# Two more merge gate tiles ahead of the first weighted sum, and output tiles that begin with the dense half

## The chip, the cores and the metric

One core of one Trainium2 chip. The metric is the time of one execution in device microseconds, shown as the median of several runs; a profile is one execution of its own. PE is the matmul engine, DVE the vector engine, ACT the scalar engine, POOL and SP the other two; SP mostly issues DMAs.

## What is computed

A decoder trunk of two layers over 512 tokens of width 1024, all in float32. Cut to what matters:

```python
def hybrid_layer(x, ...):
    h = rmsnorm(x, norm_g)
    proj = h @ w_in                       # one projection feeds everything below
    ...
    o_nsa, o_pool, o_conv, o_fox = ...    # four mixers of width 256; two are attentions
    acc = None
    for i, o in enumerate((o_nsa, o_pool, o_conv, o_fox)):
        branch = (o * jax.nn.silu(gates[:, :, i])) @ w_branch[i]
        term = jax.nn.sigmoid(merge[:, :, i]) * branch      # merge: 4 x 1024 columns of proj
        acc = term if acc is None else acc + term
    return x + acc @ w_out

def reference(x, ...):
    for l in range(DEPTH):
        x = hybrid_layer(x, ...)
    return rmsnorm(x, final_norm_g)
```

## The kernel before, in words

**Tiles.** Activations lie with features on the 128 partitions and the 512 tokens along the columns. A weight tile is 128 x 1024: eight blocks of 128 input features for 128 output features, 512 KB. To keep float32 accuracy every operand is held in two parts, a high one and the rest: ACT makes the high part (`split`, L70), DVE the rest (L71, or L74 with a scale), and each product is three matmuls: high times high, high weight times rest, rest of the weight times high. So `dense` (L286) makes one output tile of 128 features by 24 matmuls (L299) into a bank `ps_d` (three of them). The evacuation that it gets as `evac` is put into a background list and runs between later matmuls.

**Weights.** `Stream` (L88) holds the order in which the weight tiles are loaded and used. Raw tiles go into three buffers `wr` by DMAs that SP issues (L168); the split parts lie in `wh` and `wl`, two buffers each. Ahead of the merge, `ws.more()` (L152) lends it more raw buffers: one in the space of the tables `rope`, three in that of `V`, the attention's values.

**A layer in order.** Projections and gates; then 12 attention units, written out by a plan by hand (L1190 on): scores (`S`, L648 and L649), softmax on DVE and ACT (L651 to L663), transposes (`T`, L672), values (`PV`, L694), reading of the bank `ps_o` by ACT and DVE (L717, L718), and at a head pair's end its branch input `y` (L702 to L707). Between these steps `FILL` = 7 matmuls of a generator, `filler` (L1156), are issued: more projections, at the end the merge gates of the first output tile, `for i in range(4)` at L1170. A merge gate tile is a `dense` whose evacuation, `ev_merge` (L807), scales (L320) and applies a tanh on ACT (L813).

**The weighted sum** is made in two ways. The first 512 of its 1024 features, the *dense half*, go tile by tile: `branches(m)` (L818) takes the four gates of tile m, multiplies each by its branch (24 matmuls, L828, into `ps_s` and `ps_pt`; L833, L837) and splits the sum into `st`. The loop at L1212 makes the four gates of tile m, then `branches(m)`; `m` = 0 has had its gates in the filler. The other 512 features come out of `merge` (L951) with the tokens on the partitions, by a scheme that saves matmuls (seven products instead of eight); at its end (L1032 to L1040) PE turns them round by 16 transposes (L1036) and they are split into `y`. Its first weight tiles are prepared ahead.

**The output projection.** Layer 0: for each of eight tiles a `dense` over `(ah, al)`, the eight features of the sum, and the residual added by `ev_out` (L1232). `dense` takes the eight features in order, the high weight's two products first, so its 14 first matmuls need features of the dense half (0 to 3) and of the turned half (4 to 7). The last layer makes the eight tiles twice, for 256 tokens each (L1264 on, `ev_last` L1252), so that the last norm and the stores of the first half of the tokens lie beside the second half's matmuls; its eight weight tiles are loaded and split twice (L105).

**What sets the order.** The program is written in the order above, but the tile framework puts the instructions of each engine into an order of its own at build time, from the dependences, the buffers and its own estimate of times. On the chip each engine works through its list in order. So a change of the source's order moves instructions only as far as that list shows.

## Time and profile before

| | us |
|---|---|
| median of 3 runs | 966.85 |
| lowest and highest | 966.73, 968.93 |
| the profiled execution | 966.74 |
| its span, first to last instruction | 964.9 |
| PE busy | 939.8 (97%) |
| DVE busy | 715.6 (74%) |
| ACT busy | 522.0 (54%) |
| mean granted clock of PE | 0.993 of full |

The busy times are shares of the span; PE's is long because a matmul's end is modelled. "Granted clock" is the share of its 2.4 GHz that PE was given; 0.5 is 1.2 GHz.

### The profile page before, as it was taken

What the parts mean: (1) busy time and instruction counts of PE and PEld (TensorE: products, weight loads), DVE (VectorE), ACT (ScalarE), POOL (GpSimd) and SP (SyncE); (2) the same over time, 40 slices, a digit from 0 to 9 for tenths busy, and PEclk for the clock granted to TensorE, in tenths of its full rate; (3) what the DMA queues carried; (4) which work ended last, traced back from release to release, by engine and by line L of the source; (5) the groups of instructions that cost most, each with busy time, mean ns of one, the idle gap of its engine ahead of it and who ended that gap; (6) DMA issues with size and microseconds to landing.
All of it is one profiled execution on the core that took longest, in us unless ns stands there. A gap on an engine that the chain in (4) does not pass through costs nothing.

```text
span 964.9 us, 12942 instructions
## 1 busy us (share of the span) xinstructions
PE 939.8 (97%) x4728; PEld 797.9 (83%) x4728; DVE 715.6 (74%) x1397; ACT 522.0 (54%) x912; POOL 31.1 (3%) x45
## 2 busy tenths in 40 slices
PE   7999999999999999999999999999998999999896
PEld 5988888888778888887889888888886888888796
DVE  6694689986887677775568549998778868676765
ACT  7295475665644454544327537566655544545363
POOL 0000000000000001000100000000000000000010
PEclk9999999999999999999999999999999999999998
DMA  6253222132254667644514322221312655686253
GB/s 263 78 173 111 86 80 76 57 110 66 66 160 146 166 205 196 187 140 148 188 62 164 120 88 87 66 69 64 109 66 98 192 141 171 211 214 210 70 181 129
DMA packets 39904, 125.81 MB, mean 130 GB/s; under 512 B 4496, under 2 KB 6560, under 8 KB 39840
## 3 DMA queue, kind: packets, MB, share of 16 engines
q1 hardware_dynamic: 36000, 113.43, 35.4%
q0 software_dynamic: 2976, 10.50, 5.5%
q10 hardware_dynamic: 864, 1.05, 0.3%
q8 instruction: 37, 0.61, 0.3%
q14 instruction: 27, 0.22, 0.1%
HBM read 120.77 MB, written 4.19 MB: 130 GB/s over the span
## 4 chain that ended last, share of the span: by engine, by line
PE 93%; DVE 3%; DMA 1%; ACT 1%; issue 1%; POOL 0%; DVEq 0%; SPq 0%; ACTq 0%; POOLq 0%
PE ps_d L299 55%; PE ps_d L984 9%; PE ps_s L984 5%; PE ps_o L694 3%; PE ps_pt L672 2%; PE ps_pt L984 2%; PE ps_s L828 2%; PE ps_pt L1022 2%; PE ps_s L550 2%; PE ps_pt L550 2%; PE ps_s L649 1%; PE ps_pt L828 1%; PE ps_s L648 1%; PE ps_o L1022 1%; PE ps_d L1022 1%; PE ps_o L411 1%
## 5 line engine op out<-in xcount | busy, mean ns | idle before, releaser
L299 PE MATMUL ps_d<-xh,wh 128*128 128x512 f32 x632 | 249.8, 396 | 9.1 <-ACT xh L73 6.7
L299 PE MATMUL ps_d<-xl,wh 128*128 128x512 f32 x632 | 249.7, 395 | 0.0
L70 ACT ACTIVATE wh<-wr 128x1024 fp32r<-128x1024 f32 (+2 forms) x136 | 140.9, 1039 | 170.0 <-PE ps_d L299 76.5
L71 DVE TENSOR_TENSOR wl<-wr,wh 128x1024 fp32r<-128x1024 f32 (+2 forms) x136 | 162.7, 1200 | 48.2 <-ACT wh L70 47.8
L299 PE MATMUL ps_d<-xh,wl 128*128 128x512 f32 x632 | 172.7, 391 | 0.0
L299 PEld LDWEIGHTS ps_d<-xh,wh 128*128 128x128 f32 x632 | 119.6, 189 | 32.8 <-ACT xh L73 6.7
L299 PEld LDWEIGHTS ps_d<-xl,wh 128*128 128x128 f32 x632 | 119.5, 189 | 24.1 <-DVE xl L74 1.2
L299 PEld LDWEIGHTS ps_d<-xh,wl 128*128 128x128 f32 x632 | 117.5, 188 | 23.4
L320 DVE TENSOR_TENSOR t<-ps_d,rstd 128x512 f32<-128x512 f32 x74 | 50.8, 686 | 36.0 <-PE ps_d L299 35.5
L653 ACT ACTIVATE p<-p,nm 128x128 f32<-128x128 f32 (+1 forms) x96 | 53.3, 556 | 26.1 <-DVE nm L651 25.4
L651 DVE CUSTOM_DVE_ANT_0 p<-ps_s,cst 128x128 f32<-128x128 f32 (+1 forms) x96 | 45.3, 484 | 14.4 <-PE ps_pt L672 7.7
L694 PE MATMUL ps_o<-ptx,V 128*128 128x256 f32 (+1 forms) x288 | 49.6, 286 | 2.4 <-DVE o L718 1.6
L70 ACT ACTIVATE ptx<-ps_pt 128x384 fp32r<-128x384 f32 (+1 forms) x72 | 37.0, 520 | 26.6 <-PE ps_o L694 11.9
L694 PEld LDWEIGHTS ps_o<-ptx,V 128*128 128x128 f32 x288 | 42.4, 191 | 6.2 <-DVE o L718 2.2
L71 DVE TENSOR_TENSOR ptx<-ps_pt,ptx 128x384 fp32r<-128x384 f32 (+1 forms) x72 | 42.0, 594 | 2.1 <-ACT ptx L70 2.0
L672 PE MATMUL ps_pt<-cst,p 128*128 128x128 f32 x240 | 40.7, 277 | 1.3 <-DVE ptx L71 0.9
L299 PE MATMUL ps_d<-y,wh 128*128 128x256 f32 (+1 forms) x192 | 40.3, 329 | 0.9 <-ACT y L73 0.9
L299 PE MATMUL ps_d<-st,wh 128*128 128x256 f32 (+1 forms) x192 | 34.2, 321 | 1.3 <-ACT wh L70 1.3
L299 PEld LDWEIGHTS ps_d<-y,wh 128*128 128x128 f32 x192 | 30.6, 197 | 3.7 <-ACT y L73 1.4
L672 PEld LDWEIGHTS ps_pt<-cst,p 128*128 128x128 f32 x240 | 28.2, 141 | 5.6 <-PE ps_o L694 1.3
L71 DVE TENSOR_TENSOR wl<-V,wh 128x1024 fp32r<-128x1024 f32 x18 | 22.0, 1224 | 14.3 <-ACT wh L70 14.1
L299 PEld LDWEIGHTS ps_d<-st,wh 128*128 128x128 f32 x192 | 28.5, 190 | 4.7 <-ACT wh L70 2.1
(341 smaller groups left out, 1725.7 us busy)
## 6 DMA issues: line engine op xcount, KB each, us to landing
wr<-in_w_all_dram SPq DMA_DIRECT2D x145, 512.0 KB, 3.3
V<-in_w_all_dram SPq DMA_DIRECT2D x26, 512.0 KB, 3.8
rope<-in_w_all_dram SPq DMA_DIRECT2D x12, 512.0 KB, 4.2
t<-in_xT_dram SPq DMA_DIRECT2D x16, 256.0 KB, 4.5
V<-in_w_all_dram POOLq DMA_DIRECT2D x8, 512.0 KB, 8.0
wr<-in_w_all_dram SPq DMA_DIRECT2D x8, 400.0 KB, 3.0
wr<-in_w_all_dram POOLq DMA_DIRECT2D x6, 512.0 KB, 6.2
ptc<-in_xT_dram SPq DMA_DIRECT2D x8, 256.0 KB, 3.3
```

The costliest lines, as they stand in the source:

```text
L70: ACT.activation(hi, src, AF.Copy)
L71: DVE.tensor_tensor(lo, src, f32(hi), ALU.subtract)
L299: PE.matmul(acc[:, :width], w, r[k][:, tok], start=(n == 0), stop=(n == 23))
L320: DVE.tensor_tensor(t, acc, state["rb"], ALU.mult)
L550: PE.matmul(accs[tt][:, 0:400], x[:, tt * 128:tt * 128 + 128], w, start=(k == 0 and a == 0), stop=(kp == 3 and kk == 1 and a == 2))
L651: DVE.tensor_tensor_reduce(out=P[:, :n], in0=s[:, :n], in1=bias, scale=1.0, scalar=3e38, op0=ALU.add, op1=ALU.min, accum_out=nm)
L653: ACT.activation(P[:, :n], P[:, :n], AF.Exp, bias=nm, scale=-1.0, accum_out=sm)
L672: PE.transpose(p[:, c:c + 128], self.P[qt][:, kb * 128:kb * 128 + 128], ident)
L694: PE.matmul(dst, V[:, kb, self.vset, :], part[:, src], start=(self.fresh and self.cmp is None and b == 0 and kb == 0 and j == 0), stop=(se ...
L828: PE.matmul(p, w[:, c], r, start=(n == 0), stop=(n == 5))
L984: PE.matmul(bank[tt], x, w[:, d], start=(opens and k == 0 and n == 0), stop=(name in ("P2", "P3", "P4") and k == 3 and n == 2), skip_group ...
L1022: PE.matmul(p, x[:, c], w[:, d], start=(n == 0), stop=(n == 5))
```

## The change

1. **Gates.** `filler` makes six merge gate tiles instead of four (`LOGITS[:4 + AHEAD]`). In the loop, `branches(m)` now comes ahead of the next four gates, so each sum has its gates and two of the following tile behind it; the last sum is preceded by two gates alone. `ws.more()` is called behind the second group of gates. The weight tiles are laid out in that order.
2. **Output tiles.** `dense` gets `early`: the 12 matmuls that need the dense half only come first, all three products, then the other 12. The first two output tiles of each layer are such; their generators (`lead`) are advanced by 12 matmuls each inside `merge`, ahead of the transposes.
3. **The last layer.** Its first two output tiles are made once for all 512 tokens; the other six for 256 at a time, as before. The sum of squares of the two tiles (`sq01`) is kept for both halves. Two weight tiles fewer are loaded.

```diff
--- before.py
+++ after.py
@@ -24,6 +24,8 @@
 ACT_NORM = ()
 HID = (9, 11, 13, 15)
 GATES = [(0, 0), (2, 0), (0, 1), (2, 1), (1, 0), (3, 0), (1, 1), (3, 1)]
+LOGITS = [(m, i) for m in range(4) for i in range(4)]
+AHEAD = 2
 BIG = 1e30
 HEAD_ROWS = (1, 3, 0, 2)
 SWAP = [(i + 8) % 16 if i < 16 else i for i in range(32)]
@@ -102,7 +104,7 @@
                                 self.added.add(len(self.order) - 1)
                     self.order += [(l, o + 9), (l, o + 8)]
                 self.order += [(l, i) for i in range(NTILE - KT, NTILE)]
-            self.order += [(L - 1, i) for i in range(NTILE - KT, NTILE)]
+            self.order += [(L - 1, i) for i in range(NTILE - KT + 2, NTILE)]
             self.n = len(self.order)
             self.loaded = self.done = self.taken = 0
             self.slots = ["wr"] * 3
@@ -283,13 +285,15 @@
                 pass
             bg.pop(0)
 
-    def dense(rhs, evac, tok=slice(0, T)):
+    def dense(rhs, evac, tok=slice(0, T), early=False):
 
         i, (wh, wl) = ws.take()
         drain(2)
         acc = psum("d", 3)
         order = [(a, k) for k in range(7) for a in (0, 1)] + [(2, k) for k in range(7)]
         order += [(a, 7) for a in range(3)]
+        if early:
+            order = [(a, k) for h in (0, 4) for b in ((0, 1), (2,)) for k in range(h, h + 4) for a in b]
         rh, rl = rhs
         width = tok.stop - tok.start
         for n, (a, k) in enumerate(order):
@@ -804,11 +808,11 @@
         yield
 
 
-    def ev_merge(i):
+    def ev_merge(m, i):
 
         def g(acc):
             t = scaled(acc)
-            state["sig"][i] = t
+            state["sig"][m, i] = t
             yield
             ACT.activation(t, t, AF.Tanh, scale=0.5)
             yield
@@ -829,7 +833,7 @@
                     n += 1
             if i == 0:
                 ws.split(i0 + 1)
-            sg = state["sig"][i]
+            sg = state["sig"].pop((m, i))
             DVE.scalar_tensor_tensor(sg, sg, 1.0, p, op0=ALU.add, op1=ALU.mult)
             if tot is None:
                 tot = sg
@@ -948,7 +952,7 @@
         merge_ahead(1)
         return ready.pop(0)
 
-    def merge(l, side, ah, al):
+    def merge(l, side, ah, al, lead):
 
         rth = sb([128, 8], "rth", 1)
         DVE.tensor_scalar(rth[:, 0:4], state["rt"], 0.5, None, op0=ALU.mult)
@@ -1029,6 +1033,13 @@
                         DVE.tensor_tensor(acc[tok], acc[tok], sg, ALU.add)
                     if tok == toks[0]:
                         merge_ahead(2)
+        state["prep"] = None
+        assert not ready
+        ws.slots = [x for x in ws.slots if x == "wr"]
+
+        for g in lead:
+            for _ in range(12):
+                next(g)
 
         for f in range(4):
             pt = psum("pt", 2)
@@ -1038,9 +1049,6 @@
             split(h, lo, pt, scale=0.5)
             ah.append(h)
             al.append(lo)
-        state["prep"] = None
-        assert not ready
-        ws.slots = [x for x in ws.slots if x == "wr"]
 
 
     nc.gpsimd.dma_start(ng, gains)
@@ -1167,8 +1175,8 @@
             yield from dense(rhs, ev_conv("x", 1))
             yield from with_mix(dense(rhs, ev_conv("c", 1)))
             yield from dense(rhs, ev_conv("b", 1))
-            for i in range(4):
-                yield from dense(rhs, ev_merge(i))
+            for m, i in LOGITS[:4 + AHEAD]:
+                yield from dense(rhs, ev_merge(m, i))
 
         def with_mix(d):
             for n, _ in enumerate(d):
@@ -1212,20 +1220,14 @@
         for m in range(4):
             if m == 1:
                 ws.more()
-            if m:
-                for i in range(4):
-                    for n, _ in enumerate(dense(rhs, ev_merge(i))):
-                        if n % 12 == 11 and steps:
-                            next(side)
-                            steps -= 1
             a, b = branches(m)
+            for mi in LOGITS[4 * m + 4 + AHEAD:4 * m + 8 + AHEAD]:
+                for n, _ in enumerate(dense(rhs, ev_merge(*mi))):
+                    if n % 12 == 11 and steps:
+                        next(side)
+                        steps -= 1
             ah.append(a)
             al.append(b)
-        merge(l, side, ah, al)
-        if l + 1 < L:
-            par = load_par(l + 1)
-
-
         if l + 1 < L:
             def ev_out(m, xres):
                 def g(acc):
@@ -1236,34 +1238,54 @@
                     yield
                 return g
 
-            for m in range(KT):
+            def project(m):
                 xres = temp()
                 nc.sync.dma_start(xres, (xT.rearrange("(k p) t -> k p t", p=128) if l == 0 else x1d)[m])
-                run(dense((ah, al), ev_out(m, xres)))
-            drain()
-
-
-    xn = []
-    for m in range(KT):
-        xres = sb([128, T], "xh", 8)
-        nc.sync.dma_start(xres, x1d[m])
-        xn.append(xres)
-
-    def ev_last(m, c):
-        def g(acc):
-            x = xn[m][:, c]
-            DVE.tensor_tensor(x, acc[:, :T // 2], x, ALU.add)
-            add_square(x, m)
-            yield
-            if m < KT - 1:
-                ACT.activation(x, x, AF.Copy, scale=ng[:, 16 + m:17 + m])
-            yield
-        return g
+                yield from dense((ah, al), ev_out(m, xres), early=m < 2)
+        else:
+            xn = []
+
+            def ev_last(m, c):
+                def g(acc):
+                    x = xn[m][:, c]
+                    if m == 2:
+                        state["sq"] = state["sq01"][:, c]
+                    DVE.tensor_tensor(x, acc[:, :c.stop - c.start], x, ALU.add)
+                    add_square(x, m)
+                    if m == 1:
+                        state["sq01"] = state["sq"]
+                    yield
+                    if m < KT - 1:
+                        ACT.activation(x, x, AF.Copy, scale=ng[:, 16 + m:17 + m])
+                    yield
+                return g
+
+            def project(m, half=0):
+                if half == 0:
+                    xres = sb([128, T], "xh", 8)
+                    nc.sync.dma_start(xres, x1d[m])
+                    xn.append(xres)
+
+                c = slice(half * T // 2, half * T // 2 + T // 2) if m > 1 else slice(0, T)
+                yield from dense((ah, al), ev_last(m, c), c, early=m < 2)
+
+        lead = [project(m) for m in range(2)]
+        merge(l, side, ah, al, lead)
+        if l + 1 < L:
+            par = load_par(l + 1)
+
+
+        for g in lead:
+            run(g)
+        for m in range(2, KT):
+            run(project(m))
+        drain()
+
 
     for half in range(2):
         c = slice(half * T // 2, half * T // 2 + T // 2)
-        for m in range(KT):
-            run(dense((ah, al), ev_last(m, c), c))
+        for m in range(2, KT) if half else ():
+            run(project(m, half))
         drain()
         _, rb = stats(T // 2, keep=True)
         x = xn[KT - 1][:, c]
@@ -1355,8 +1377,9 @@
             tiles += [feat(run(s + 128 * h)) for s in (652, 908, 1420, 1164)]
         pairs = lambda m: [m[256 * j:256 * j + 256].reshape(2, 128, 512).transpose(1, 0, 2).reshape(128, 1024)
                            for j in range(len(m) // 256)]
+        logit = [feat(run(3472 + 1024 * i + 128 * m)) for m, i in LOGITS]
         for m in range(4):
-            tiles += [feat(run(3472 + 1024 * i + 128 * m)) for i in range(4)]
+            tiles += logit[4 * m + (AHEAD if m else 0):4 * m + 4 + AHEAD]
             tiles.append(a["w_branch"][l].reshape(8, 128, 1024)[:, :, m * 128:m * 128 + 128]
                          .transpose(1, 0, 2).reshape(128, 1024))
         for bp in range(2):
```

The order of the instructions on an engine, before and now, at three places. In the rows, `xh`, `xl` are the parts of the normalised input, `wh`, `wl` those of a weight tile, `ptx` and `V` probabilities and values, `y` branch inputs (at the output: the turned half of the sum), `st` the dense half of the sum.

**PE, layer 1, behind the last score matmuls** (before: `L648`, `L649` scores, `L828` sums). Before, at the place where the value matmuls of the last two units begin:

```order
L672 MATMUL ps_pt<-cst,p 128x128 x2
L694 MATMUL ps_o<-ptx,V 128x256
L694 MATMUL ps_o<-ptx,V 128x128 x2
L828 MATMUL ps_s<-y,wh 128x512 x3
L828 MATMUL ps_s<-y,wl 128x512
L828 MATMUL ps_s<-y,wh 128x512 x2
L828 MATMUL ps_s<-y,wl 128x512
L672 MATMUL ps_pt<-cst,p 128x128 x2
```

Now, at the same place (`L303` gates, `L832` sums):

```order
L698 MATMUL ps_o<-ptx,V 128x256 x2
L698 MATMUL ps_o<-ptx,V 128x128 x2
L676 MATMUL ps_pt<-cst,p 128x128 x3
L698 MATMUL ps_o<-ptx,V 128x256 x4
L303 MATMUL ps_d<-xh,wh 128x512
L303 MATMUL ps_d<-xl,wh 128x512
L303 MATMUL ps_d<-xh,wl 128x512
L832 MATMUL ps_s<-y,wh 128x512 x2
L832 MATMUL ps_s<-y,wl 128x512
L698 MATMUL ps_o<-ptx,V 128x256 x2
L698 MATMUL ps_o<-ptx,V 128x128 x2
L676 MATMUL ps_pt<-cst,p 128x128 x7
```

Ahead of the first row now stand 21 matmuls of one gate tile, and behind the last row 24 of another; before, no gate tile stood there, only sums.

**PE, the output of the last layer**, from the last matmul row of `merge` on. Before:

```order
L1022 MATMUL ps_pt<-wl,y 128x512
L299 MATMUL ps_d<-st,wh 128x256 x16
L1036 MATMUL ps_pt<-cst,p 128x128 x8
L299 MATMUL ps_d<-y,wh 128x256 x2
L1036 MATMUL ps_pt<-cst,p 128x128 x4
L299 MATMUL ps_d<-y,wh 128x256 x4
L1036 MATMUL ps_pt<-cst,p 128x128 x4
L299 MATMUL ps_d<-y,wh 128x256 x5
L299 MATMUL ps_d<-st,wl 128x256 x4
```

Now:

```order
L1026 MATMUL ps_pt<-wl,y 128x512
L303 MATMUL ps_d<-st,wh 128x512 x8
L303 MATMUL ps_d<-st,wl 128x512 x4
L303 MATMUL ps_d<-st,wh 128x512 x8
L1047 MATMUL ps_pt<-cst,p 128x128 x4
L303 MATMUL ps_d<-st,wl 128x512 x4
L1047 MATMUL ps_pt<-cst,p 128x128 x4
L303 MATMUL ps_d<-y,wh 128x512 x2
L1047 MATMUL ps_pt<-cst,p 128x128 x4
L303 MATMUL ps_d<-y,wh 128x512 x4
L1047 MATMUL ps_pt<-cst,p 128x128 x4
L303 MATMUL ps_d<-y,wh 128x512 x9
```

The two tiles' matmuls with `st` stand ahead of the transposes with all three products, 512 columns wide; before, 16 of 256 columns stood there.

**ACT, layer 1, around the last value matmul.** Before:

```order
L70 ACTIVATE ptx<-ps_pt 128x384
L717 ACTIVATE o<-ps_o 64x512
L705 ACTIVATE y<-o 128x512
L70 ACTIVATE ptx<-V 128x1024
L70 ACTIVATE wh<-wr 128x1024 x2
```

Now:

```order
L72 ACTIVATE ptx<-ps_pt 128x384
L721 ACTIVATE o<-ps_o 64x512
L817 ACTIVATE t<-t 128x512
L709 ACTIVATE y<-o 128x512
L72 ACTIVATE ptx<-V 128x1024
L817 ACTIVATE t<-t 128x512
L72 ACTIVATE wh<-wr 128x1024 x2
```

A tanh (`L817`) now stands between the split of the merge tile in `V` and the splits of the next two gates' weights.

## Rows read from the trace of the kernel before

**Rows 1.** The page: busy time by engine; shares of the chain by engine
```profile
PE 939.8 (97%) x4728; PEld 797.9 (83%) x4728; DVE 715.6 (74%) x1397; ACT 522.0 (54%) x912; POOL 31.1 (3%) x45
...
PE 93%; DVE 3%; DMA 1%; ACT 1%; issue 1%; POOL 0%; DVEq 0%; SPq 0%; ACTq 0%; POOLq 0%
```

**Rows 2.** Table of stretches: us, busy by engine (instructions), PE's granted clock, DMA share, GB/s
```profile
254.51:270.63 16.12, 14.12 (x87) 11.78 (x86) 14.08 (x33) 9.45 (x19) 0.00 (x0) 1.00 0.18 49
270.63:278.66 8.03, 6.02 (x27) 4.23 (x26) 7.12 (x11) 3.28 (x5) 0.00 (x0) 1.00 0.56 198
724.18:740.53 16.35, 14.46 (x78) 11.75 (x77) 13.36 (x32) 8.84 (x18) 0.00 (x0) 0.90 0.16 49
740.53:747.51 6.98, 6.01 (x26) 4.22 (x25) 6.88 (x11) 3.28 (x5) 0.00 (x0) 1.00 0.62 225
431.30:478.37 47.07, 46.13 (x209) 37.52 (x208) 27.84 (x39) 18.72 (x26) 3.84 (x7) 1.00 0.48 162
900.14:954.77 54.63, 51.96 (x413) 50.84 (x412) 36.07 (x58) 30.34 (x50) 3.46 (x3) 0.97 0.42 135
732.60:735.62 3.02, 3.02 (x8) 2.31 (x9) 2.77 (x7) 0.60 (x1) 0.00 (x0) 0.52 0.35 85
906.51:909.43 2.92, 2.92 (x15) 2.92 (x14) 0.89 (x2) 1.19 (x2) 0.00 (x0) 0.50 0.00 0
```

**Rows 3.** Groups by line on PE, 254.5 to 270.62: values and transposes
```profile
L694 PE MATMUL ps_o<-ptx,V 128*128 128x256 f32 (+1 forms) x36 | 6.2, 289 | 1.4 <-DVE o L718 1.3
...
L672 PE MATMUL ps_pt<-cst,p 128*128 128x128 f32 x20 | 3.3, 277 | 0.3 <-DVE ptx L71 0.3
```

**Rows 4.** PE in order of time, steady pieces: start us, us, line and operation, count
```profile
236.26 1.02 PE L694 MATMUL ps_o<-ptx,V 128*128 128x256 f32 x7
237.11 0.62 PE L672 MATMUL ps_pt<-cst,p 128*128 128x128 f32 x4
237.49 0.42 PE L648 MATMUL ps_s<-st 128*128 128x384 f32 x1
...
252.25 1.75 PE L299 MATMUL ps_d<-xh,wl 128*128 128x512 f32 x7
253.83 0.39 PE L299 MATMUL ps_d<-xh,wh 128*128 128x512 f32 x1
...
920.58 1.12 PE L299 MATMUL ps_d<-st,wh 128*128 128x256 f32 x8
921.54 0.52 PE L299 MATMUL ps_d<-y,wh 128*128 128x256 f32 x3
```

**Rows 5.** PE in order of time, layer 0's attention end: [idle before, releaser]
```profile
261.75 0.84 PE L694 MATMUL ps_o<-ptx,V 128*128 128x256 f32 x5 [1.29 <-DVE o L718]
...
278.66 0.50 PE L299 MATMUL ps_d<-xh,wh 128*128 128x512 f32 x1 [1.73 <-ACT wh L70]
```

**Rows 6.** ACT and PE in order of time, layer 0: weight splits, a tanh, a gate's first matmul
```profile
247.29 1.06 ACT L70 ACTIVATE wh<-wr 128x1024 fp32r<-128x1024 f32 x1 [0.63 <-ACT p L653]
...
255.50 0.61 ACT L813 ACTIVATE t<-t 128x512 f32<-128x512 f32 x1
...
276.60 1.06 ACT L70 ACTIVATE ptx<-V 128x1024 fp32r<-128x1024 f32 x1 [2.06 <-DMA V<-in_w_all_dram]
277.57 1.99 ACT L70 ACTIVATE wh<-wr 128x1024 fp32r<-128x1024 f32 x2
...
248.99 0.44 PE L299 MATMUL ps_d<-xh,wh 128*128 128x512 f32 x1
```

**Rows 7.** PE and ACT in order of time, the output of layer 1
```profile
904.09 0.66 PE L1036 MATMUL ps_pt<-cst,p 128*128 128x128 f32 x4 [1.16 <-DVE p L1029]
905.22 0.51 PE L299 MATMUL ps_d<-y,wh 128*128 128x256 f32 x2 [0.47 <-ACT y L73]
...
912.97 1.21 PE L299 MATMUL ps_d<-st,wh 128*128 128x256 f32 x8 [0.79 <-ACT wh L70]
...
911.86 2.01 ACT L70 ACTIVATE wh<-wr 128x1024 fp32r<-128x1024 f32 x2 [2.65 <-PE ps_d L299]
```

## The prediction

> **What bounds the kernel now.** I read the busy shares and the chain that ended last first: PE is busy 97% of the span and makes up 93% of the chain [rows 1]. A change of order gains only where PE waits or runs slowly, so I then read PE's rows in order of time and looked for gaps. Leaving out the start and the last 10 us, they sit in four places: the end of the attention in each layer, and the first output tiles of each layer. The table of stretches [rows 2] gives the length of each place; the groups by line [rows 3] give what PE does there; steady rows [rows 4] give the pace without a wait. The reader should see that busy time is no measure here (a matmul's end is modelled), so I take start-to-start paces: seven 512-column matmuls in 1.58 us (0.226 each, I use 0.227), eight 256-column ones in 0.96 (0.12), four transposes in 0.38 (0.095), seven value matmuls of mixed width in 0.85 (0.12).
>
> Layer 0, end of attention up to the last value matmul: 16.12 us for 87 matmuls [rows 2]: 36 value (4.3), 20 transposes (1.9), 24 of the weighted sums (5.45), 6 scores (about 1.0) and one gate matmul (0.2): 12.9. So 3.2 us are waits, the longest 1.29 for DVE's reading of the value bank [rows 5]. Layer 1: 16.35 us for 31, 20, 24, 2 and 1, which is 11.7: 4.6 us, of which 1.43 is the clock. Between 732.60 and 735.62 it is granted at about half (1.2 instead of 2.4 GHz), and seven sum matmuls take 3.02 us instead of 1.59 [rows 2]. Before it fell, PE had been waiting off and on for DVE and ACT.
>
> Behind the last value matmul there are 24 sum matmuls (5.45 us) in 8.03 us of layer 0 and in 6.98 of layer 1: 2.6 and 1.5 us of wait. PE is idle 1.73 us until ACT has split the next gate's weights [rows 5], and ACT is late because ahead of that split it holds the split of a merge tile that waits 2.06 us for its DMA [rows 6]. That DMA writes the space of the attention's values, so it starts only behind the last value matmul.
>
> Output, layer 0: 47.07 us for 192 matmuls of 512 (43.6) and 16 transposes (1.5): 2.0 us of waits. Output, layer 1: 54.63 us for 384 of 256 columns (46.1), 16 transposes (1.5) and some 1.1 of small matmuls of the norm: 5.9 us of waits. They are 1.16 for the last sum on DVE, 0.47 for ACT's first split, 0.79 for the weights of the third tile [rows 7], and 1.46 for the clock: from 906.51 to 909.43 nine matmuls of 256 and four transposes take 2.92 us at half clock, 1.46 at full [rows 2].
>
> **The change part by part.** *Gate tiles.* The number of gate, sum and attention matmuls stays; no DMA is added, the weights are only laid out in another order. In layer 0 one gate tile (24 matmuls, 5.45 us) now stands behind the last score matmul and one more among the attention steps before; in layer 1 two (10.9 us) stand behind it. The order rows show them ahead of value matmuls and transposes that waited before. 5.45 and 10.9 us of ready work are more than the 3.2 and 4.6 us of wait, so most of these go; what is late next is the same DVE chain, which had 14.08 of 16.12 us busy in layer 0 [rows 2], now spread over a longer stretch. I leave 0.8 us per layer (bounds: nothing stays, all stays). In layer 1 the clock's 1.43 us go with the waits.
> Behind the last value matmul nothing gets better. The merge tile's load still starts there, and ACT's queue now holds one tanh more, for the last gate, between that tile's split and the next gate's weights: 0.61 us [rows 6]. Layer 0: 0.6 longer, all of it waiting. In layer 1 three more sum matmuls (0.7 us) moved behind the last value matmul, which fill the 0.6. Bounds: nothing, if the tanh finds room while ACT waits for the load; 1.2, if the evacuation that DVE must do for it also holds back the last attention rows.
> Layer 0: 3.2 − 0.8 − 0.6 = 1.8 us gained (bounds 3.2 gained to 1.2 lost). Layer 1: 4.6 − 0.8 = 3.8 (4.6 gained to 1.2 lost).
> The later request for the merge's extra buffers costs nothing: their loads wait for the last value matmul in either order.
>
> *Output tiles, layer 0.* 24 matmuls of the dense half (5.45 us, four of them between the first transposes) instead of 16 (3.6) now lie ahead of the last transposes, so the wait for the last DVE sum is covered. Of the 2.0 us I leave 0.8: the 0.47 that ACT needs for the first split, since only tiles that need the turned half are left then, and 0.3 for a transpose bank. Gain 1.2 (bounds 0 to 2.0).
>
> *Output tiles, layer 1.* Two tiles become 48 matmuls of 512 (10.9 us) in place of 96 of 256 (11.5): 0.6 gained. Two weight loads with their splits on ACT and DVE fall away; they lay beside PE, which had no gap from 912.97 on, so they count nothing. The 5.45 us of dense-half work cover the sum, which came 3.95 us after the merge's last matmul (900.14 to 904.09) [rows 7]. The third tile's weights were late because ACT may overwrite the first tile's buffer only when PE has read it for the last time; now nine matmuls of 512 (2.0 us) lie behind that reading, against 1.0 for the split, so the 0.79 goes. Of 5.9 us I leave 1.2, the same two waits as in layer 0 and some start-up. Gain 0.6 + 4.7 = 5.3 (bounds 3.8, if the clock falls all the same, to 6.5). The end behind the last matmul is unchanged.
>
> Sum: 1.8 + 3.8 + 1.2 + 5.3 = 12.1 us. The profiled execution took 966.74 us (span 964.9), which is 0.11 below the median of the three runs, too little to correct for: 954.6 us, a span of about 952.8.
>
> *A rule against this.* The rows tie the clock to many short gaps: it fell in both places behind gaps of at most 1.3 us, and stayed at full level (1.00) in the stretch with the 1.73 us gap that came after steady work [rows 2, 5]. The Trainium skill, "TensorE: Matmul & The Clock Gate", section "HAM oscillation — how this bites in real kernels", explains a lowered clock by one long idle gap between bursts. The next section there, on PSUM-queue cycling, knows the form with frequent short gaps, as the rows have it. If only long gaps mattered, what falls here would not depend on these waits and would stay, and the sum would give 957.5 instead of 954.6.
>
> **The rivals.**
> 1. *The clock falls anyway.* For it: after the change short waits remain in the same places, 2 to 3 us behind the last value matmul and about 1 us at the output. Against it: layer 0 has such waits today and keeps 1.00 there [rows 2]. Price 1.43 + 1.46 = 2.9 us: 957.5.
> 2. *The gate tiles only shift the chain* (for these places, that the change doesn't do what it says). PE is in order; if the value matmuls and transposes behind the gates start later by as much as the gates take, and the chain through DVE and ACT is as long as now, both tails gain nothing. For it: DVE is busy 87% in the layer 0 stretch. Against it: ptx, sums and probabilities of two units are under way at once, and their DVE work goes on under the gates. Only the outputs gain, 6.5: 960.2.
> 3. *Slower: one weight buffer for all gates.* Of the two buffers for split weights, the first sum's tile holds one from early on; every gate of the attention's end passes through the other. So ACT's split (1.06 us) must fit between a gate's last reading and the next gate's first matmul. Today it does: ACT starts at 247.29, PE comes to the next gate at 248.99 [rows 6]. In the new order nine such turns stand in the two layers, with some 1.6 to 3 us of other PE work in each. It decides where ACT comes to the split more than half a microsecond late, behind a softmax step. If all nine turns fail by a whole split and its hand-over (about 1.3 us, an estimate), 11.7 us go: 966.3, no change. If the clock also falls at four of them (1.45 each), 972.1.
>
> **How the numbers follow.** Chances: forecast 0.72, rival 1 0.12, rival 2 0.09, rival 3 without the clock 0.04, with it 0.03. Single terms may miss by 1 to 3 us each, and two or three together reach 951 below; above, the range goes to 959.5, which takes in rival 1 with one term missed and leaves out rivals 2 and 3 (0.16). A measurement of this kernel tells about 0.3%, 2.9 us, from no change: faster means below 963.9. Forecast and rivals 1 and 2 are faster, 0.93; rival 3 gives 0.04 same and 0.03 slower.
>
> **What would show it.** Right: in PE's rows no gap over about 0.5 us between the last scores and the last value matmul; still a gap of 1.5 to 3.5 us ahead of the first gate behind the sums, with ACT's weight split as releaser; 24 first matmuls of 512 columns at the output without a wait; granted clock 1.00 in both layers' tails and at the output; layer 1's output about 49.3 us long instead of 54.6. Wrong: new gaps of over 1 us ahead of gate matmuls among the attention steps, released by ACT (rival 3); a tail as long as now plus the gates moved in (rival 2); clock rows of half in stretches with little idle (rival 1); a gap ahead of the third output tile.

## The result, and the profile after

| | before | after |
|---|---|---|
| median, us | 967.89 (4 runs, 966.73 to 969.71) | 954.65 (4 runs, 954.59 to 957.72) |
| the profiled execution, us (span) | 966.74 (964.9) | 954.59 (952.8) |

The ratio is 0.9869, with a 95% interval of 0.9842 to 0.9896: some 1.3% faster; 954.6 us had been forecast. (The functions that the text ahead places at L88, L152, L818 and L1156 stand at L91, L135, L817 and L1158, as printed.) After's lines are a few higher than before's: gates and outputs L303, value matmuls L698, sums L832, tanh L817.

Before's executions fall into two groups: of the 37 taken beside the experiments below, 25 lie at 965.2 to 967.7 us with a mean granted clock of 0.992 to 0.994, and 12 at 968.6 to 970.0 with 0.989 to 0.991; two of the four above are of each, and the profile that the forecast was read from is of the first, from which the change gains 12.1 us, against 13.2 between the medians.

The page of after, busy times and chain, beside [rows 1]: the work is nearly the same, PE's share of the chain rose from 93 to 96%.

```profile
PE 933.3 (98%) x4680; PEld 792.0 (83%) x4680; DVE 714.3 (75%) x1392; ACT 520.2 (55%) x906; POOL 31.1 (3%) x45
...
PE 96%; DVE 2%; ACT 1%; DMA 1%; issue 0%; POOL 0%; DVEq 0%; SPq 0%; ACTq 0%; POOLq 0%
```

The table of stretches of after, beside [rows 2]: layer 0 from the last score steps to the last value matmuls, and from there to the next gate; the same two of layer 1; the output of layer 0 and of layer 1 (us, busy by engine, PE's granted clock, DMA share, GB/s).

```profile
256.69:279.23 22.54, 22.50 (x122) 19.05 (x120) 17.30 (x35) 10.56 (x20) 0.00 (x0) 1.00 0.24 83
279.23:286.98 7.75, 6.33 (x28) 4.50 (x26) 7.62 (x13) 4.44 (x7) 0.00 (x0) 1.00 0.53 203
722.97:743.08 20.11, 20.11 (x107) 17.09 (x106) 14.39 (x25) 8.78 (x15) 0.00 (x0) 1.00 0.23 70
743.08:751.86 8.78, 6.93 (x32) 5.15 (x30) 8.55 (x14) 4.44 (x7) 0.00 (x0) 1.00 0.65 231
428.75:475.09 46.34, 45.87 (x210) 37.55 (x208) 28.01 (x39) 18.82 (x26) 3.86 (x7) 1.00 0.47 165
893.62:943.19 49.57, 49.10 (x366) 46.39 (x365) 33.15 (x53) 27.79 (x44) 3.46 (x3) 1.00 0.39 128
```

The reader should see three things: PE fills the stretches up to the last value matmuls, the clock is 1.00 in every row (0.90 and 0.97 in two of [rows 2]), and both stretches behind the value matmuls still have over a microsecond without PE. These are all of PE's rows with an idle time ahead of them, start and last 10 us left out:

```profile
248.08 0.56 PE L698 MATMUL ps_o<-ptx,V 128*128 128x256 f32 x3 [0.57 <-DVE ptx L73]
...
285.25 0.50 PE L832 MATMUL ps_s<-y,wh 128*128 128x512 f32 x1 [0.90 <-DVE y L711]
...
286.98 0.50 PE L303 MATMUL ps_d<-xh,wh 128*128 128x512 f32 x1 [0.53 <-ACT wh L72]
...
435.73 0.73 PE L303 MATMUL ps_d<-y,wh 128*128 128x512 f32 x2 [0.47 <-ACT y L75]
...
749.06 0.50 PE L832 MATMUL ps_s<-y,wh 128*128 128x512 f32 x1 [0.24 <-DVE y L711]
...
751.86 0.50 PE L303 MATMUL ps_d<-xh,wh 128*128 128x512 f32 x1 [1.60 <-ACT wh L72]
...
900.60 0.73 PE L303 MATMUL ps_d<-y,wh 128*128 128x512 f32 x2 [0.47 <-ACT y L75]
```

Beside before's list [rows 5, 7], the waits between the last scores and the last value matmul are gone, and so are those of the output but for the 0.47 for ACT's first split. The first row, 0.57 us ahead of the last scores of layer 0, is new; before had one of 0.17 us in that region, at 239.69.

To say where a run gained, I cut every profiled execution at the same instructions: the first score matmul of layer 0, the merge's first matmul in each layer, the first output matmul of each, the end of each output, the end of the span. Lengths in us, each the difference of two starts in PE's rows in order of time. The stretches up to a merge hold more than the attention's end; what one gains is called its tail's below, since nearly all of before's gaps in it lie there. (ptx_first is left out, since its order mixes the merge with its neighbours.)

| run | up to first scores | layer 0 to merge | merge | output 0 | layer 1 to merge | merge | output 1 | end |
|---|---|---|---|---|---|---|---|---|
| before | 116.11 | 217.09 | 98.10 | 47.07 | 323.67 | 98.10 | 54.63 | 10.13 |
| after | 116.64 | 214.00 | 98.11 | 46.34 | 320.42 | 98.11 | 49.57 | 9.61 |
| gates_only | 116.63 | 214.28 | 98.10 | 47.08 | 320.21 | 98.11 | 54.65 | 10.04 |
| out_only | 115.88 | 220.32 | 98.11 | 46.34 | 323.92 | 98.16 | 49.57 | 10.10 |
| early_only | 115.56 | 214.11 | 98.11 | 46.34 | 320.19 | 98.28 | 52.14 | 9.97 |
| wide_only | 115.74 | 214.03 | 98.09 | 47.11 | 321.81 | 98.09 | 50.36 | 9.57 |
| ahead1 | 116.74 | 218.37 | 98.09 | 46.34 | 319.66 | 98.09 | 49.57 | 9.94 |
| ahead3 | 116.16 | 214.06 | 101.11 | 46.34 | 319.64 | 99.18 | 49.55 | 9.66 |
| ptx_late | 115.66 | 214.75 | 101.64 | 46.33 | 321.00 | 101.54 | 49.57 | 10.11 |
| after_again | 116.40 | 214.08 | 98.11 | 46.34 | 322.57 | 98.10 | 49.57 | 10.13 |
| ptx_hold | 116.06 | 214.05 | 98.11 | 46.34 | 319.28 | 98.12 | 49.54 | 9.60 |
| wide4 | 115.75 | 214.06 | 98.09 | 46.34 | 320.29 | 98.10 | 49.38 | 9.29 |
| hold_wide4 | 115.73 | 214.01 | 98.09 | 46.32 | 319.26 | 98.88 | 49.37 | 9.34 |

Before to after: 3.09 us in layer 0's tail, 3.25 in layer 1's, 0.73 and 5.06 in the outputs. A start longer by 0.53 and an end shorter by 0.52 cancel; over the other programs and executions these two wander by about as much (after_again, the same program, has an end of 10.13), so I don't count them as the change's.

### The profile page after: what moved, and what is told of

It reads as the page before. It is cut to its first block, busy times and chain, and to the rows that moved or that the text cites. A ratio compares the mean times of both kernels' runs of the same rounds, so it can differ in the third digit from the quotient of the medians.

```text
span 952.8 us, 12820 instructions
## 1 busy us (share of the span) xinstructions
PE 933.3 (98%) x4680; PEld 792.0 (83%) x4680; DVE 714.3 (75%) x1392; ACT 520.2 (55%) x906; POOL 31.1 (3%) x45
## 4 chain that ended last, share of the span: by engine, by line
PE 96%; DVE 2%; ACT 1%; DMA 1%; issue 0%; POOL 0%; DVEq 0%; SPq 0%; ACTq 0%; POOLq 0%
PE ps_d L303 56%; PE ps_d L988 9%; PE ps_s L988 5%; PE ps_o L698 3%; PE ps_pt L676 3%; PE ps_pt L988 2%; PE ps_pt L1026 2%; PE ps_s L554 2%; PE ps_pt L554 2%; PE ps_s L832 2%; PE ps_s L653 2%; PE ps_s L652 1%; PE ps_pt L832 1%; PE ps_o L1026 1%; PE ps_d L1026 1%; PE ps_o L415 1%
## 5 line engine op out<-in xcount | busy, mean ns | idle before, releaser
L303 PE MATMUL ps_d<-xh,wh 128*128 128x512 f32 x632 | 250.3, 397 | 9.0 <-ACT xh L75 6.8
L303 PE MATMUL ps_d<-xl,wh 128*128 128x512 f32 x632 | 250.2, 396 | 0.0
L72 ACT ACTIVATE wh<-wr 128x1024 fp32r<-128x1024 f32 (+2 forms) x134 | 138.9, 1038 | 155.2 <-PE ps_d L303 71.5
L73 DVE TENSOR_TENSOR wl<-wr,wh 128x1024 fp32r<-128x1024 f32 (+2 forms) x134 | 160.4, 1199 | 54.1 <-ACT wh L72 52.2
L303 PE MATMUL ps_d<-xh,wl 128*128 128x512 f32 x632 | 174.1, 392 | 0.0
L303 PEld LDWEIGHTS ps_d<-xh,wh 128*128 128x128 f32 x632 | 119.9, 190 | 32.9 <-ACT xh L75 6.8
L303 PEld LDWEIGHTS ps_d<-xl,wh 128*128 128x128 f32 x632 | 119.5, 189 | 23.8 <-DVE xl L76 1.2
L303 PEld LDWEIGHTS ps_d<-xh,wl 128*128 128x128 f32 x632 | 117.5, 188 | 23.1
L324 DVE TENSOR_TENSOR t<-ps_d,rstd 128x512 f32<-128x512 f32 x74 | 50.7, 686 | 26.7 <-PE ps_d L303 26.3
L698 PE MATMUL ps_o<-ptx,V 128*128 128x256 f32 (+1 forms) x288 | 48.8, 282 | 0.6 <-DVE ptx L73 0.6
L698 PEld LDWEIGHTS ps_o<-ptx,V 128*128 128x128 f32 x288 | 42.4, 190 | 3.6 <-DVE ptx L73 0.8
L303 PE MATMUL ps_d<-y,wh 128*128 128x256 f32 (+1 forms) x176 | 38.0, 336 | 0.9 <-ACT y L75 0.9
L303 PE MATMUL ps_d<-st,wh 128*128 128x256 f32 (+1 forms) x176 | 33.5, 332 | 0.0
L72 ACT ACTIVATE wh<-V 128x1024 fp32r<-128x1024 f32 x18 | 19.1, 1061 | 22.7 <-PE ps_s L832 7.2
L303 PEld LDWEIGHTS ps_d<-y,wh 128*128 128x128 f32 x176 | 27.9, 190 | 4.2 <-ACT y L75 1.4
```

Of the source, the lines that this page charges most:

```text
L72: ACT.activation(hi, src, AF.Copy)
L73: DVE.tensor_tensor(lo, src, f32(hi), ALU.subtract)
L303: PE.matmul(acc[:, :width], w, r[k][:, tok], start=(n == 0), stop=(n == 23))
L324: DVE.tensor_tensor(t, acc, state["rb"], ALU.mult)
L698: PE.matmul(dst, V[:, kb, self.vset, :], part[:, src], start=(self.fresh and self.cmp is None and b == 0 and kb == 0 and j == 0), stop=(se ...
```

## The experiments

Each edit is against after unless it says otherwise. Medians stand with the ratio to before and its 95% interval.

**gates_only**, the gates alone

(against before; the output tiles stay as they are there)

```diff
...
-            for i in range(4):
-                yield from dense(rhs, ev_merge(i))
+            for m, i in LOGITS[:4 + AHEAD]:
+                yield from dense(rhs, ev_merge(m, i))
...
+            for mi in LOGITS[4 * m + 4 + AHEAD:4 * m + 8 + AHEAD]:
+                for n, _ in enumerate(dense(rhs, ev_merge(*mi))):
...
```

> The gate part of the change alone: two more gate tiles ahead of the first sum, output tiles as before. Between the profiles of before and after, layer 0's part up to the merge became 3.1 us shorter from the first scores on, layer 1's tail 3.3, and the start was 0.5 longer. My theory, that the gates cover PE's waits in the tails: these two gains stay, the output of layer 1 is about 54.6 us long with its half-clock stretch, total about 966.7 - 6.3 = 960.4 us. Rival, that the gates only shift the chain and the gain comes of the output tiles: about 966 us, with both merges starting less than 1 us earlier than before.

959.89 us (0.9918, 0.9904 to 0.9933). Both tails gain as in after (214.28, 320.21), both outputs are before's (47.08, 54.65). The rival that the gates only shift the chain falls.

**out_only**, the output tiles alone:

```diff
-AHEAD = 2
+AHEAD = 0
```

(`ws.more()` then comes one group of gates later than in before, as in after.)

> The output part alone: the gates stand as before (four ahead of the first sum), the output tiles as after. My theory: layer 0's output 46.3 us instead of 47.1, layer 1's 49.6 instead of 54.6, tails as before with the half-clock stretch in layer 1's tail, total about 966.7 - 0.7 - 5.1 = 960.9 us. Rival, that the outputs gain only because PE comes to them at a full clock from a better tail: layer 1's output 51 us or more, half clock in it, total 962.4 or more.

963.59 us (0.9959, 0.9944 to 0.9973). The outputs are after's to the hundredth (46.34, 49.57), so they owe nothing to the tails; and the later `ws.more()` alone gains nothing in them. But the total is 2.7 us above the forecast: layer 0's tail is 3.2 us longer than before's. PE's gaps there are before's (0.32, 1.29, 0.30, 0.29, 1.80 against 0.32, 1.29, 0.30, 0.28, 1.73, two of them in [rows 5]); what differs is the clock. The table of stretches of this run, layer 0's tail and then layer 1's:

```profile
264.00:270.00 6.00, 6.00 (x29) 5.11 (x30) 4.78 (x11) 2.49 (x5) 0.00 (x0) 0.74 0.16 45
276.00:282.00 6.00, 3.91 (x14) 2.56 (x13) 5.12 (x8) 2.95 (x3) 0.00 (x0) 0.90 0.37 124
282.00:288.00 6.00, 6.00 (x23) 4.79 (x23) 5.90 (x11) 2.38 (x6) 0.92 (x1) 0.82 0.63 195
732.00:738.00 6.00, 4.94 (x18) 3.63 (x19) 5.65 (x16) 2.42 (x5) 0.00 (x0) 0.73 0.16 46
```

At half rate a share of 1 - c of a stretch is lost when the mean is c: 1.56 us in the first row, 0.60 and 1.08 in the next two, 3.2 together. So the gates can be worth more than the waits that they fill: without them the clock fell in both tails of this execution; with them (after, gates_only) PE has no gap between the last scores and the last value matmul for it to fall behind.

**early_only**, the order of the lead tiles without the 512 columns:

```diff
...
-                c = slice(half * T // 2, half * T // 2 + T // 2) if m > 1 else slice(0, T)
-                yield from dense((ah, al), ev_last(m, c), c, early=m < 2)
+                c = slice(half * T // 2, half * T // 2 + T // 2)
+                yield from dense((ah, al), ev_last(m, c), c, early=m < 2 and half == 0)
...
```

> As after, but the last layer makes all eight output tiles for 256 tokens at a time; the first two of the first half still begin with the dense half. My theory: 12 first matmuls of each lead tile are now 256 wide, so 24 of 0.12 us (2.9) lie ahead of the turned half instead of 5.45, while the last sum comes 3.95 us after the merge's last matmul: about 1 us of wait comes back, 0.6 us of matmul time comes back, and two splits more lie on ACT: total 956 to 957.5 us. If the clock falls again, 957.5 to 959. Rival, that the order alone made the gain and the width nothing: within 0.7 us of after, 954.6 to 955.3.

956.45 us (0.9885, 0.9870 to 0.9900), as forecast. Layer 1's output takes 52.14 us, 2.57 more than after's, with these gaps in PE's rows:

```profile
895.94 0.74 PE L303 MATMUL ps_d<-st,wl 128*128 128x256 f32 x4 [0.36 <-DVE wl L73]
...
897.66 0.51 PE L303 MATMUL ps_d<-y,wh 128*128 128x256 f32 x2 [0.47 <-ACT y L75]
...
898.39 0.66 PE L1047 MATMUL ps_pt<-cst,p 128*128 128x128 f32 x4 [0.22 <-DVE y L76]
...
901.37 0.39 PE L303 MATMUL ps_d<-y,wh 128*128 128x256 f32 x1 [0.18 <-DVE y L76]
```

The clock does not fall. The lead work is used up before ACT and DVE have the second tile's weights and the turned features.

**wide_only**, the 512 columns without the order:

```diff
-            for _ in range(12):
+            for _ in range(8):
...
-                yield from dense((ah, al), ev_last(m, c), c, early=m < 2)
+                yield from dense((ah, al), ev_last(m, c), c)
```

(and the line of layer 0, with `ev_out`, alike)

> As after, but the first two output tiles keep the old order of their 24 matmuls; the lead in the merge is 8 each, the high products with the dense half, and the last layer's two tiles are still 512 wide. 16 x 0.227 = 3.6 us of lead work instead of 5.45. My theory: layer 0's output as before, 47.1 us (0.7 longer than after); layer 1's 50 to 51.5 (after 49.6), with some 0.3 to 1 us of wait for the last sum and 0.5 for the third tile's weights: 955.8 to 957.3 us. If the clock falls at the output: 957.3 to 958.8. Rival, that the order of the products counts nothing: 954.6 to 955.2.

955.41 us (0.9881, 0.9867 to 0.9896), just under the forecast; the stretches are as forecast: 47.11 and 50.36, each 0.8 longer than after's, with a wait of 0.47 for the third tile's weights in both. So of layer 1's 5.06 us the width alone brings 4.3 (54.65 to 50.36), the order alone 2.5 (to 52.14), both 5.1: they overlap, since wide lead tiles are also more cover. In layer 0, where all is 512 wide, the order brings the whole 0.7.

**ahead1** and **ahead3**, one and three gates ahead:

```diff
-AHEAD = 2
+AHEAD = 1
```

(and 3 in the second)

> As after, with one gate tile ahead instead of two. The tails' waits ahead of the last value matmul were 3.2 and 4.6 us, one gate tile is 5.45 us of ready work. If any work of that length will do: 955 to 956.5 us, no half clock in the tails. If both are needed (one gate is used up before the last evacuations, and the short waits come back): gaps of 0.5 us and more ahead of value matmuls, half clock in one or both tails, 957 to 960.

958.33 us (0.9906, 0.9889 to 0.9922). Layer 1's tail needs no more than this (319.66), layer 0's does: 218.37, which is 1.3 longer than before's. With one gate less in hand PE comes to the sums before ACT has written `y`, and behind that gap it runs at half clock (0.67 from 269.70 to 274.00). PE in order of time:

```profile
265.93 0.84 PE L698 MATMUL ps_o<-ptx,V 128*128 128x256 f32 x5 [0.26 <-DVE o L722]
...
269.70 1.65 PE L832 MATMUL ps_s<-y,wh 128*128 128x512 f32 x3 [1.97 <-ACT y L709]
```

> As after, with three gate tiles ahead. If the tails ahead of the last value matmul are already full, as after's rows say, and the rest is bound by the load into the values' space, nothing is left for a third gate: 954.2 to 955.5 us, gaps behind the last value matmul as in after. Rival, that more ready work also covers the wait for the last branch input: 952.5 to 953.7.

958.24 us (0.9914, 0.9888 to 0.9939): neither case. The tails are as in after or better (214.06, 319.64), but the merges, 98.1 us in after, take 101.11 and 99.18, with new waits for weights, as PE's rows show:

```profile
350.33 0.50 PE L988 MATMUL ps_d<-wl,st 128*128 128x512 f32 x1 [2.67 <-DVE wl L73]
...
815.48 0.50 PE L988 MATMUL ps_d<-wl,st 128*128 128x512 f32 x1 [0.79 <-DVE wl L73]
```

Why that split comes late there I did not follow up.

**ptx_first**, the merge tile that ACT splits in the tail taken from other space:

```diff
-            if next(count) % 3 == 2:
+            if next(count) % 3 == 0:
```

> As after, but of the merge's weight tiles the first, fourth, seventh ... go to the buffer ptx instead of the third, sixth, ...: the tile that ACT splits ahead of the next gate's weights then lies in the space of the rotary tables, free early, and not in that of the attention's values. My theory: behind the last value matmul ACT waits 0.94 and 2.01 us for a DMA into the values' space, and this holds the next gate's split: the gaps of 0.53 and 1.60 us ahead of the gates go, total 952.5 us. Rival, that the gate's weights would be late anyway (the raw tile's own load, or DVE's rest behind the evacuations): the gaps stay with DVE or a DMA as releaser, total 954.2 to 954.9.

960.27 us (0.9918, 0.9902 to 0.9935): slower than after and than both cases that I had named; my theory was half of it. ACT waits for no DMA there, but the tile's rest now stands on DVE among the last steps of the attention (DVE in order of time):

```profile
279.71 1.22 DVE L73 TENSOR_TENSOR ptx<-rope,ptx 128x1024 fp32r<-128x1024 f32 x1
280.85 0.68 DVE L324 TENSOR_TENSOR t<-ps_d,rstd 128x512 f32<-128x512 f32 x1
281.56 0.69 DVE L722 TENSOR_TENSOR o<-ps_o,o 64x512 f32<-64x512 f32 x1
...
286.49 0.68 DVE L711 TENSOR_TENSOR y<-o,y 128x512 fp32r<-128x512 f32 x1
```

The sums wait 1.61 us for that last `y` (0.90 in after), and the clock falls behind it in both layers (0.72 over 6 us, 1.7 us each).

**ptx_late**, the same tile in `wh` and `wl`:

```diff
...
-            if next(count) % 3 == 2:
+            seen.append(r)
+            if next(count) % 3 == 2 and len(seen) > 3:
```

> As after, but the merge's third weight tile is split into the buffers wh and wl and not into ptx, so that no split of a merge tile can stand among the attention's last steps, on ACT or on DVE. In the run that split this tile earlier from other space, its rest on DVE (1.22 us) came ahead of the last attention evacuation and the sums waited for that. My theory now: the wait behind the last value matmul has two links, ACT's wait for the DMA into the values' space, and DVE's chain to the last branch input; with the split gone from both engines the gaps of 0.53 and 1.60 us ahead of the gates go, those of 0.90 and 0.24 for the branch input stay: 952.5 us, or up to 953.5 if the merge's third tile, now in a buffer that is reused at once, costs up to 0.5 us per layer. Rival, that DVE alone is the bound there: the gate's weights are late all the same, released by DVE, 954 to 955. If the clock falls behind the gaps that are left, 956 or more.

964.90 us (0.9968, 0.9955 to 0.9980), far above all that I had forecast. Behind the value matmuls it does what the theory says: the gaps ahead of the gates are 0.46 and 0.45, those for `y` 0.89 and 0.24. But the merge, short of a buffer, loses 3.5 us per layer, and its first matmul waits 0.59 and 1.58 us more, which counts in the tails. PE at the start of layer 0's merge:

```profile
330.41 0.50 PE L991 MATMUL ps_d<-wh,xh 128*128 128x512 f32 x1 [0.59 <-ACT wh L72]
...
337.72 0.50 PE L991 MATMUL ps_d<-wl,xh 128*128 128x512 f32 x1 [1.64 <-DVE wl L73]
```

**after_again**, **ptx_hold** and **wide4**, on one chip. `ptx_hold` leaves the tile where it was and makes its split depend on the first sum:

```diff
+        if m == 0:
+            state["one"] = sb([128, 1], "one", 1)
+            DVE.tensor_scalar(state["one"], f32(lo[:, 0:1]), 0.0, 1.0, op0=ALU.mult, op1=ALU.add)
...
+            if n == 2:
+                ACT.activation(hi, r, AF.Copy, scale=state["one"])
+                DVE.tensor_tensor(lo, r, f32(hi), ALU.subtract)
```

`wide4` changes the five places where the last layer tells its first two output tiles from the rest, so that it is four tiles.

> The changed kernel once more, beside the two runs that follow. Both theories: 954.6 to 955.6 us by its other times (its profile's start to the first scores was 116.64 us, of other runs 115.6 to 115.9, so the start may move by up to 1 us from one program or execution to the next).

> As after, but the split of the merge's third weight tile multiplies by a 1.0 that is worked out from the first sum's result: it stays in the buffer ptx and in the values' space, and can only come behind the first sum, on ACT and on DVE. My theory, from the run with that tile in wh: the gap behind the sums shrinks from 0.53 and 1.60 us to about 0.45 in both layers, the gaps for the branch input (0.90, 0.24) stay, and since the merge keeps its third buffer the merge's waits of that run (0.6 to 1.6, 0.24 and 1.64 us per layer) don't come: 1.2 us less than after, 953.0 to 953.8 by its first times. Rival, that the split is late for the merge when it comes behind the sum: new gaps at the merge's start, 954.5 to 957. If the two numbers behind the point are the same as after, the tile's place was no cause: 954.6.

> As after, with the first four output tiles of the last layer 512 wide instead of two (two of them begin with the dense half, as in after). By the paces, a tile of 24 x 0.227 = 5.45 us takes the place of 48 x 0.12 = 5.76: 0.3 us less for each of two tiles, and two weight loads with their splits fewer: 0.6 us less than after, 954.0 by its first times. Rival: the norm and the stores of the first half lie beside the second half's matmuls, now 96 of 256 columns (11.5 us) instead of 144 (17.3); if ACT's and DVE's splits, evacuations and the norm don't fit there, gaps open ahead of the last tiles, 955 to 957.

after_again: 955.48 us (0.9867, 0.9848 to 0.9887; 953.61 to 957.23). Its profiled execution is the one of 957.23, and shows the wait that ptx_hold is meant to remove at its worst. PE in order of time, layer 1:

```profile
752.22 0.51 PE L303 MATMUL ps_d<-xh,wh 128*128 128x512 f32 x1 [2.13 <-ACT wh L72]
```

Behind it the clock falls; the stretch that follows:

```profile
752.22:755.90 3.68, 3.68 (x11) 2.90 (x12) 3.68 (x5) 0.90 (x1) 0.01 (x1) 0.64 0.41 146
```

ptx_hold: 954.14 us (0.9853, 0.9838 to 0.9869; 953.60 to 954.56). Layer 1's tail is 319.28 us, 1.14 less than after's, the merge keeps its 98.1. ACT in order of time, and PE's gate:

```profile
747.90 0.63 ACT L817 ACTIVATE t<-t 128x512 f32<-128x512 f32 x1 [1.17 <-DVE t L324]
749.06 2.01 ACT L72 ACTIVATE wh<-wr 128x1024 fp32r<-128x1024 f32 x2 [0.52 <-PE ps_s L832]
...
750.17 0.50 PE L303 MATMUL ps_d<-xh,wh 128*128 128x512 f32 x1 [0.44 <-ACT wh L72]
```

The total lies 0.3 us above the forecast. So the merge tile's split, waiting for its DMA, did hold the gate's weights. What is late next is PE itself: the split now starts when PE has done with the sums.

wide4: 954.44 us (0.9862, 0.9842 to 0.9883). Output 1 is 0.2 us shorter instead of 0.6, since PE now waits 0.30 us at its end for DVE's last sum of squares. But behind that a wait of after's for ACT is gone, so output 1 and the end together are 0.5 us shorter (58.67 instead of 59.18). PE in wide4, and in after:

```profile
942.01 0.58 PE L235 MATMUL ps_o<-onesf,p 128*128 128x1 f32 x4 [0.30 <-DVE p L250]
...
944.31 0.61 PE L235 MATMUL ps_o<-onesf,t 128*128 128x1 f32 x4 [0.62 <-ACT t L241]
```

**hold_wide4**, both edits:

> The two edits that each left a shorter stretch, together: the third merge tile held behind the first sum, and four output tiles 512 wide in the last layer. By the stretches of the profiles: layer 1's tail 1.1 us shorter than in after (319.3 instead of 320.4 from the end of layer 0 to the merge), the output 0.2 (49.4 instead of 49.6): 1.2 to 1.4 us less than after where the clock does not fall, 953.3 to 954.0, with no execution over 955. If the wide tiles bring nothing once the tail is repaired (the last sum of squares on DVE now ends behind the last matmul): the same as the held tile alone, 954.1.

953.79 us (0.9870, 0.9850 to 0.9890; 952.88 to 955.14). One execution is over the 955 that I had set as a limit, and layer 1's merge is 0.8 us longer, with a new wait of 0.49 for a split's rest on DVE. The last three versions and after can't be told apart by their intervals against before; what is shown is the 1.1 us in layer 1's tail with the split held back.

## Why the prediction was right, point by point

The mechanism held: PE's waits were covered, and the clock's loss went with them. That the total came so near is luck. The four parts, forecast and measured: layer 0's tail 1.8 and 3.09 us, layer 1's 3.8 and 3.25, the outputs 1.2 and 0.73, 5.3 and 5.06. The misses cancel, and after_again's median for the same program is 955.48.

**Gate tiles, ahead of the last value matmul: right.** Forecast: 3.2 and 4.6 us of wait become 0.8 each, a gain of 2.4 and 3.8. Measured: layer 0's tail gained 3.09, of which 0.68 lie behind the last value matmul (below), so 2.41; layer 1's gained 3.25 although 1.39 were lost behind it, 0.68 of that by three sum matmuls that moved there, so 3.96. Layer 1's half clock is gone with the waits. What I left standing (0.8 us for the DVE chain) isn't where I had it: no row of that stretch has an idle time, and the one new wait, 0.57 us for DVE, stands earlier in layer 0.

**Behind the last value matmul: the step that failed.** I had this stretch 0.6 us longer in both layers, by a tanh on ACT; in layer 1 the moved sum matmuls were to fill that. From the last value row to the next gate it was 8.43 us before and 7.75 after in layer 0, 7.39 and 8.78 in layer 1. Before's last value rows, layer 0 and 1, and ACT's split in layer 1 (that of layer 0 is in [rows 6]):

```profile
270.23 0.57 PE L694 MATMUL ps_o<-ptx,V 128*128 128x256 f32 x4
...
740.12 0.57 PE L694 MATMUL ps_o<-ptx,V 128*128 128x256 f32 x4
...
745.45 1.06 ACT L70 ACTIVATE ptx<-V 128x1024 fp32r<-128x1024 f32 x1 [1.01 <-DMA V<-in_w_all_dram]
```

ACT's rows in after, layer 0 and 1:

```profile
284.40 1.06 ACT L72 ACTIVATE ptx<-V 128x1024 fp32r<-128x1024 f32 x1 [0.94 <-DMA V<-in_w_all_dram]
285.37 0.62 ACT L817 ACTIVATE t<-t 128x512 f32<-128x512 f32 x1
285.89 1.99 ACT L72 ACTIVATE wh<-wr 128x1024 fp32r<-128x1024 f32 x2
...
749.28 1.06 ACT L72 ACTIVATE ptx<-V 128x1024 fp32r<-128x1024 f32 x1 [2.01 <-DMA V<-in_w_all_dram]
750.25 0.61 ACT L817 ACTIVATE t<-t 128x512 f32<-128x512 f32 x1
750.76 1.99 ACT L72 ACTIVATE wh<-wr 128x1024 fp32r<-128x1024 f32 x2
```

The tanh does stand on the path, for 0.5 us. But the start of the split that waits for the DMA moved by more: 6.37 us behind the last value row before, 5.17 after in layer 0; 5.33 and 6.20 in layer 1. The DMA rows show it. The four loads into `V` around this place in before, layer 0 and layer 1 (KB each, median us from issue to landing):

```profile
V<-in_w_all_dram SPq DMA_DIRECT2D x4, 512.0 KB, 4.3
...
V<-in_w_all_dram SPq DMA_DIRECT2D x4, 512.0 KB, 3.8
```

The same in after, layer 0 and layer 1:

```profile
V<-in_w_all_dram SPq DMA_DIRECT2D x4, 512.0 KB, 3.8
...
V<-in_w_all_dram SPq DMA_DIRECT2D x4, 512.0 KB, 4.8
wr<-in_w_all_dram SPq DMA_DIRECT2D x1, 512.0 KB, 3.5
```

SP issues the first three within 1 us of each other, right behind the last value matmul, and the split starts when the second has landed: that load alone takes 5.3 us in before and 4.2 in after in layer 0, 4.3 and 5.3 in layer 1. I had taken the landing as fixed; it moves by a microsecond, and in layer 1 also from one execution of the program to another (2.13 us of gap in after_again instead of 1.60). Why is open. In after's layer 1 another weight load of 512 KB, issued 2 us ahead, runs beside them, and the gap is 1.35 us or more in all six profiles that have it so and leave the split where it is; but no run moved that load alone, and in before's layer 0 no weight load runs beside them and the second takes as long. The two layers' errors, 1.3 us too pessimistic and 0.7 too optimistic, nearly cancel. The other bound that I named showed too: two gate evacuations on DVE (L324, at 280.07 and 283.92) stand ahead of the last `y` of layer 0, and the sums wait 0.90 us for it, 0.28 in before:

```profile
275.73 0.50 PE L828 MATMUL ps_s<-y,wh 128*128 128x512 f32 x1 [0.28 <-DVE y L707]
```

Layer 1 has the same two (743.88, 747.72), but there three more sum matmuls lie ahead, and 0.24 is left.

**Outputs: right, the parts uneven.** Layer 1: 5.06 of 5.3. But the width is worth far more than the 0.6 of its pace, because it is cover as well (wide_only). Layer 0: 0.73 of 1.2. I had 2.0 us of waits there by the pace, but before's rows have only two of 0.47 in it; what fell is the one for the third tile's weights, with the slower matmuls around it. The other, for ACT's first split, stayed in both layers, as forecast. The one that fell, in before:

```profile
445.60 2.11 PE L299 MATMUL ps_d<-st,wh 128*128 128x512 f32 x8 [0.47 <-ACT wh L70]
```

**Rivals.** The clock stayed at 1.00 in after's profile (rival 1), the gates don't only shift the chain (rival 2), and no gate waits for its one buffer among the attention's steps (rival 3). Rival 1 was nearer than its chance said: after_again, the same program, shows the clock falling behind layer 1's sums, 957.23 us, and one of after's own four executions took 957.72 at a mean clock of 0.994 (the others 0.997 and 0.998). That both are near its price of 957.5 is chance: the price was for falls in the two old places, layer 1's tail ahead of the last value matmul and its output, and in after_again's profile both are at 1.00. There 2.15 us more than in after come of layer 1's tail, 0.53 of them by the longer gap.

## What to carry to other kernels

Fill a tail of short waits with ready work on the engine that bounds, and count its clock among the gain; but look at what stays in the queues behind it. A split or evacuation that an automatic order has pulled forward, and that waits for a transfer, holds everything behind it on its in-order engine: give it a data dependence on something later, rather than another buffer or place, which here cost more than the wait. Cut each trace at the same instructions: stretches equal to the hundredth show what an edit did not touch, where totals wander by a microsecond.

## What the runs showed of the hardware that I had not expected

The clock's fall could not be read from the gaps. In layer 0's tail the same five gaps left it at 1.00 in before [rows 2, 5] and lowered it twice in out_only, which took 3.2 us. Ahead of the first gate behind the sums there is one gap each, with a smaller one (0.24 or 0.28 us, for `y`) some 3 us ahead of it and steady work otherwise. It left the clock at 1.00 with 1.35 (gates_only), 1.42 (early_only), 1.48 (wide4), 1.60 (after) and 1.73 us (before), and lowered it with 1.40 (wide_only, 321.81 us against 320.2 in early_only) and 2.13 (after_again). The longest gap of all between the first scores and the last 10 us, ahead3's 2.67 us in the merge, did not lower it. In my reasons I had used layer 0's 1.00 as evidence for safety; it was one outcome of two. The Trainium skill, "TensorE: Matmul & The Clock Gate", section "HAM oscillation — how this bites in real kernels", has the clock lowered by one long wait between bursts. Its waits are longer than any of these, so no run here shows that case; here shorter ones lowered the clock too, in some executions. Its next section, on frequent short idle times, fits the tails better, but doesn't say why 1.40 us lowered it in wide_only and 1.60 in after did not.
